# A feed-forward stage's gate and up products: product order inside a unit, and early tiles finished in turns with whole tiles

## The chip, the cores and the metric

The kernel runs on one core of a Trainium2 chip. The metric is device time in microseconds for one execution. The core has five engines, each with its own queue of instructions: TensorE (PE; its weight loads are shown as PEld), VectorE (DVE), ScalarE (ACT), GpSimd (POOL) and SyncE (SP), which issues the DMAs. They wait for each other by semaphores.

## The reference

Two layers of a decoder trunk on 512 tokens of width 1024, all in float32. Each layer has a feed-forward half-step, token mixing, a second feed-forward half-step and a gated per-layer embedding:

```python
def swiglu(x, w_in, w_out):
    gate, up = jnp.split(x @ w_in, 2, axis=-1)
    return (jax.nn.silu(gate) * up) @ w_out

for l in range(DEPTH):                                   # DEPTH = 2
    x = x + 0.5 * rms_norm(swiglu(rms_norm(x, ln_ffn1_pre[l]), w_ffn1_in[l], w_ffn1_out[l]), ln_ffn1_post[l])
    x = x + rms_norm(token_mixing(...), ln_mix_post[l])
    x = x + 0.5 * rms_norm(swiglu(rms_norm(x, ln_ffn2_pre[l]), w_ffn2_in[l], w_ffn2_out[l]), ln_ffn2_post[l])
    gate = jax.nn.sigmoid(rms_norm(x, ln_ple_pre[l]) @ w_ple_gate[l])
    x = x + rms_norm(gate * (p[l] @ w_ple_proj[l]), ln_ple_post[l])
```

The hidden width is 2816, so `x @ w_in` is 512 x 1024 times 1024 x 5632. The change lies in this product and in the SwiGLU behind it, four times in a run.

## The kernel before

**The stage.** `ffn(l, w, after)` computes gate and up for 22 tiles of 128 hidden channels (m = 0 to 21), then `ffn_out` multiplies by `w_out`. For one tile, gate and up (two rows of blocks), the halves of the 1024 inputs (two columns of blocks) and the halves L and H of the 512 tokens make a 2 x 2 by 2 x 2 block product. It is done with seven block products in place of eight, numbered 1 to 7 in `right`, from sums of weight blocks and sums of token blocks. Products 1 and 2 use the gate's plain weights, 4 uses a part of the up weights, 7 and 5 use the two halves of a first weight sum (`sx`, split into the tile w75), 6 and 3 those of a second sum (`sy`, split into w63) that is built from the first. Products 4, 6 and 7 read the token sums `tx`.

**One product.** Each float32 operand is split in two parts of type fp32r: ScalarE copies the high part (L141), VectorE subtracts to get the low part (L142). `mm3` (L169 to L171) multiplies high by high, high by low and low by high. A product is 4 x 3 = 12 matmuls of 256 columns. Its first two matmuls need the high part of the weights alone, the third needs the low part.

**Early and whole tiles.** While the normalized tokens of a stage are still being turned (`turn`, transposes named xtp), TensorE has only a part of the tokens. For the first G = 8 tiles products 1 and 2 are done in that time (`one` and `two`) from the weights w1; their sum is kept in `gates`. The seven products of these tiles are finished later by `unit(m, ...)`, which does 3 to 7 alone. I call these the early units, 0 to 7. For tiles 8 to 21 `gate` first does products 1 and 2 from a split of the gate's weights (w12) and then `unit` does the rest: whole units.

**VectorE in a unit.** L386 makes the first sum; L388 and L389 make the second; L142 makes the low parts of w75, w63, the weights of product 4 (w4) and, in a whole unit, w12. L397 adds product 6, L400 adds products 7 and 5, L403 (whole units) adds product 2, L405 adds product 3, L406 and L409 finish up, L413 multiplies by the Silu of the gate that ScalarE made (L407).

**Loads and buffers.** The raw weights (wr) come by DMA from SP's queue into slots of the pool `q`; the first three tiles' are loaded ahead. Split weights have six buffers, the sums two, PSUM banks are taken in a fixed cycle (`mmoa` for p12 and p4, `brrr` for p63 and p75).

**Who sets the order.** The source's order is a start only. The kernel is built with `schedule_with_timeline_sim=True`: a scheduler lays out the instructions of each engine from its own estimate of their times. So the rows of a unit are mixed with those of its neighbours, and a change in one place can move rows elsewhere. What each engine runs is then fixed.

Of the kernel before, what the change touches and what calls it, by code (L numbers as in the profile page):

```python
# [20 lines left out]
NM = DFF // 128  # L21
EPS = 1e-6
SLOT = 2048
NQ, NH, NW = 6, 6, 3
G, GF = 8, 3
BANKS = {"m": 2, "r": 3}
MAINL, AUXL = "mmoa", "brrr"

# [44 lines left out]
class Trunk:  # L73
# [57 lines left out]
    def bank(self, tag, name):  # L131
        return self.ps.tile([128, 512], F32, tag=tag, name=name, bufs=BANKS.get(tag, 1))

# [67 lines left out]
    def prenorm(self, t, gain, ffn=False):  # L201
        nc = self.nc
        v_, a_, g_ = nc.vector, nc.scalar, nc.gpsimd
        hs = [slice(0, 512), slice(512, 1024)]
        ss = [self.ssq(self.x[:, t, h], "ss_pre", dve=self.first and i == 1) for i, h in enumerate(hs)]
        r = self.rms(ss)
        xn = self.tmp.tile([128, D], F32, tag="xn", name="xn", bufs=1)
        for h in hs:
            v_.scalar_tensor_tensor(xn[:, h], self.x[:, t, h], r, gain[:, h], ALU.mult, ALU.mult)
        return lambda: self.turn(t, xn, ffn)  # L210

    def turn(self, t, xn, ffn):
        nc = self.nc
        v_, a_, g_ = nc.vector, nc.scalar, nc.gpsimd
# [119 lines left out]
    def ffn(self, l, w, after):  # L334


        nc, tc = self.nc, self.tc
        v_, a_, g_ = nc.vector, nc.scalar, nc.gpsimd
        post = self.gain(f"ln_ffn{w}_post", l)
        xs = (self.xh, self.xl)  # L340
        L, H = slice(0, 256), slice(256, 512)
        plain = lambda ks, ts: [q[:, ks, ts] for q in xs]
        tx = [[q[:, 0], q[:, 1]] for q in self.tx]
        k1, k2 = slice(0, 4), slice(4, 8)
        right = {1: plain(k1, L), 2: plain(k2, L), 3: plain(k2, H), 4: tx[2], 5: plain(k1, H), 6: tx[0], 7: tx[1]}
        hs = []

        lo, hi = slice(0, 512), slice(512, 1024)

        def product(n, q, out, first=True, last=True):  # L350
            for k in range(4):
                self.mm3(out, [a[:, k * 128:(k + 1) * 128] for a in q], [b[:, k] for b in right[n]],
                         first and k == 0, last and k == 3, not (first and last))


        places = lambda m: (L, H) if m % 2 else (H, L)
        early = {}

        def one(m):
            pa = self.mm_tile("p12")  # L360
            if m % 4 == 0:
                self.ffn_a = self.slot("h", [4, 512], "gates")
            early[m] = pa, self.ffn_a[:, m % 4]
            product(1, self.cut(self.ffn_w1[m], lo), pa[:, L], True, False)
            a_.activation(self.ffn_a[:, m % 4, places(m)[1]], pa[:, L], AF.Copy)

        def two(m):

            pa, a = early[m]
            product(2, self.cut(self.ffn_w1[m], hi), pa[:, L], False, True)  # L370
            a_.activation(a[:, places(m)[0]], pa[:, L], AF.Copy)

        def left(m):
            r = self.ffn_raw[m] if m < GF else self.ffn_load(l, w, [m])[0]
            if m < G:
                return r, *early[m]
            return r, self.mm_tile("p12"), self.tmp.tile([128, S], F32, tag="tb0", name="gate", bufs=4)

        def gate(m, pa, a, q):
            product(1, self.cut(q, lo), pa[:, L])  # L380
            product(2, self.cut(q, hi), pa[:, H])
            a_.activation(a[:, (H, L)[m % 2]], pa[:, L], AF.Copy)

        def unit(m, r, pa, a):
            sx, sy = (self.wraw.tile([128, 1024], F32, tag="raw", name="ws") for _ in range(2))
            v_.tensor_tensor(sx.rearrange("p (i c) -> p i c", i=2), r[:, :, lo],  # L386
                             r[:, 1].rearrange("p (i c) -> p i c", i=2), ALU.add)
            v_.tensor_tensor(sy[:, lo], sx[:, hi], r[:, 0, lo], ALU.add)  # L388
            v_.tensor_tensor(sy[:, hi], sy[:, lo], r[:, 0, hi], ALU.add)  # L389
            sx, sy = self.wsplit(sx, "w75"), self.wsplit(sy, "w63")  # L390
            u2 = [self.tmp.tile([128, 512], F32R, tag="sg", name="w4") for _ in range(2)]
            self.split(u2[0], u2[1], r[:, 1, hi])
            pc, pb, pd = self.aux_tile("p63"), self.aux_tile("p75"), self.mm_tile("p4")
            b = self.tmp.tile([128, S], F32, tag="tb1", name="up", bufs=2)
            P, Q = places(m)
            product(6, self.cut(sy, lo), pc[:, L])
            v_.tensor_tensor(a[:, Q], pc[:, L], a[:, Q if m < G else P], ALU.add)  # L397
            product(7, self.cut(sx, lo), pb[:, P])
            product(5, self.cut(sx, hi), pb[:, Q])
            v_.tensor_tensor(b.rearrange("p (i t) -> p i t", i=2), pb.rearrange("p (i t) -> p i t", i=2),  # L400
                             a[:, None, Q].to_broadcast([128, 2, 256]), ALU.add)
            if m >= G:
                v_.tensor_tensor(a[:, P], pa[:, H], a[:, P], ALU.add)  # L403
            product(3, self.cut(sy, hi), pc[:, H])
            v_.tensor_tensor(a[:, Q], pc[:, H], b[:, Q], ALU.add)  # L405
            v_.tensor_tensor(b[:, Q], pb[:, Q], b[:, P], ALU.add)  # L406
            a_.activation(a, a, AF.Silu)  # L407
            product(4, u2, pd[:, L])
            v_.tensor_tensor(b[:, P], b[:, P], pd[:, L], ALU.subtract)  # L409
            if m % 4 == 0:  # L410
                hs.append(self.slot("h", [8, 256], "h"))

            v_.scalar_tensor_tensor(hs[m // 4][:, m % 4 * 2:m % 4 * 2 + 2], b.rearrange("p (i t) -> p i t", i=2), -1.0,  # L413
                                    a.rearrange("p (i t) -> p i t", i=2), ALU.mult, ALU.mult)

        for m in range(G + 1):
            if m in NFL:
                self.flush(NFL[m])
            if m < G:
                one(m)  # L420
            if m:
                two(m - 1)
        self.flush()
        for m in range(NM):
            r, pa, a = left(m)
            if m >= G:
                gate(m, pa, a, self.wsplit(r[:, 0], "w12"))
            unit(m, r, pa, a)
        wo = self.ins[f"w_ffn{w}_out"]
        self.ffn_out(hs, lambda h, b: wo[l, h, b], post, 0.5, after)  # L430
# [1124 lines left out]
```

## Time and profile before

| | us |
|---|---|
| median of 3 runs (lowest to highest) | 2156.45 (2154.91 to 2157.81) |
| the profiled execution | 2158.23 |
| its span, first to last instruction | 2156.5 |
| TensorE busy | 2103.3 |
| VectorE busy | 1697.9 |
| ScalarE busy | 1015.6 |
| GpSimd busy | 219.9 |

The profile shows one execution. Times in it are microseconds from the start of the span, durations of single instructions are nanoseconds where the row says mean ns. In a row of a timeline the first number is the start, the second the duration; in brackets stands how long the engine was idle before it, and who ended that. A row of waits says which engine and line waited for which, the total, how often, and the longest. A row of a stretch gives its ends, its length, and for each engine the busy time and the number of instructions, then the clock that TensorE was granted (1.00 is full), the share of DMA time and GB/s. Names are cut to the tile's name without its number, so all seven products' PSUM tiles are "p" and all split weights "w". Matmuls overlap in the engine's pipeline: one lasts 280 ns or so, but the next starts after less than half of that.

The four feed-forward stages begin at about 15, 669, 1081 and 1735 us.

### The profile page before, as it was taken

To read this page: it belongs to the slowest core of one execution; us is meant where nothing else is said; L and a number is where in the kernel's file an instruction comes from. 1 tells how busy PE (TensorE), PEld (TensorE's weight loads), DVE (VectorE), ACT (ScalarE), POOL (GpSimd) and SP (SyncE) were. 2 spreads that over 40 slices of the span, in tenths; PEclk is the share of its full clock that TensorE was granted. 3 is DMA by queue.
4 is the path that set the end of the run, shared out by engine and by line. 5 is a ranking of instruction groups with operands and counts; after the bars stand their busy time and mean duration, and the time that the engine had idled before them with its cause. 6 is when DMAs were issued, how large, how long until landed. Compare 5 with 4: busy or idle time off the path is not lost.

```text
span 2156.5 us, 39845 instructions
## 1 busy us (share of the span) xinstructions
PE 2103.3 (98%) x16256; PEld 1953.4 (91%) x16256; DVE 1697.9 (79%) x2909; ACT 1015.6 (47%) x1685; POOL 219.9 (10%) x369
## 2 busy tenths in 40 slices
PE   7999999999999999999999999999999999999998
PEld 7999999898778999999889999998887789999996
DVE  8999977655767999977699999765557589999774
ACT  6444434446545444434564444345464464444343
POOL 1000011031211000011100000111412110000121
PEclk9999999999999999999999999999999999999999
DMA  5332124321042323225233222242220423222241
GB/s 215 120 116 99 70 87 153 116 65 55 21 155 71 137 99 118 69 79 182 92 108 125 111 79 93 86 169 94 61 64 2 157 88 138 100 97 79 82 147 66
DMA packets 72679, 219.10 MB, mean 102 GB/s; under 512 B 16304, under 2 KB 17328, under 8 KB 72496
## 3 DMA queue, kind: packets, MB, share of 16 engines
q1 hardware_dynamic: 72208, 216.03, 28.5%
q8 instruction: 128, 2.10, 0.4%
q10 hardware_dynamic: 288, 0.52, 0.1%
q14 instruction: 55, 0.45, 0.1%
HBM read 209.71 MB, written 6.82 MB: 100 GB/s over the span
## 4 chain that ended last, share of the span: by engine, by line
PE 84%; DVE 7%; ACT 4%; DMA 2%; issue 2%; POOL 1%; SPq 0%; DVEq 0%; POOLq 0%; ACTq 0%
PE y L496 21%; PE p L169 12%; PE p L171 12%; PE p L170 12%; PE pkrv L169 1%; PE pkrv L171 1%; PE pkrv L170 1%; DVE w L142 1%; PE y L171 1%; PE y L169 1%; PE y L170 1%; PE pgt L169 1%; PE pgt L171 1%; PE pgt L170 1%; PE po L1405 1%
## 5 line engine op out<-in xcount | busy, mean ns | idle before, releaser
L169 PE MATMUL p<-xh,w 128*128 128x256 f32 x1408 | 400.2, 286 | 14.1 <-DVE gates L397 5.8
L171 PE MATMUL p<-xh,w 128*128 128x256 f32 x1408 | 397.0, 284 | 3.7 <-DVE w L142 3.6
L170 PE MATMUL p<-xl,w 128*128 128x256 f32 x1408 | 398.7, 284 | 0.3 <-DVE xl L142 0.2
L169 PE MATMUL p<-tx,w 128*128 128x256 f32 x1056 | 294.2, 282 | 5.6 <-DVE ws L386 4.1
L170 PE MATMUL p<-tx,w 128*128 128x256 f32 x1056 | 292.1, 280 | 0.0
L171 PE MATMUL p<-tx,w 128*128 128x256 f32 x1056 | 289.8, 280 | 0.5 <-DVE w L142 0.5
L169 PEld LDWEIGHTS p<-xh,w 128*128 128x128 f32 x1408 | 268.8, 192 | 19.0 <-DVE gates L397 6.6
L171 PEld LDWEIGHTS p<-xh,w 128*128 128x128 f32 x1408 | 268.5, 192 | 5.1 <-DVE w L142 5.1
L170 PEld LDWEIGHTS p<-xl,w 128*128 128x128 f32 x1408 | 269.7, 192 | 1.0 <-DVE xl L142 0.9
L141 ACT ACTIVATE w<-ws 128x1024 fp32r<-128x1024 f32 x176 | 185.5, 1056 | 128.7 <-PE p L171 98.7
L142 DVE TENSOR_TENSOR w<-ws,w 128x1024 fp32r<-128x1024 f32 x176 | 214.0, 1217 | 19.4 <-ACT w L141 19.0
L169 PEld LDWEIGHTS p<-tx,w 128*128 128x128 f32 x1056 | 199.4, 189 | 8.1 <-ACT w L141 6.7
L170 PEld LDWEIGHTS p<-tx,w 128*128 128x128 f32 x1056 | 199.2, 189 | 0.0
L171 PEld LDWEIGHTS p<-tx,w 128*128 128x128 f32 x1056 | 196.3, 188 | 0.9 <-DVE w L142 0.7
L496 PE MATMUL y<-wo,hq 128*128 128x256 f32 x1536 | 193.3, 283 | 0.0
L496 PEld LDWEIGHTS y<-wo,hq 128*128 128x128 f32 x1536 | 186.4, 190 | 0.8
L141 ACT ACTIVATE w<-wr 128x512 fp32r<-128x512 f32 (+1 forms) x156 | 126.9, 816 | 108.8 <-PE p L171 61.5
L496 PE MATMUL y<-ws_r,h 128*128 128x256 f32 x672 | 158.3, 379 | 0.0
L142 DVE TENSOR_TENSOR w<-wr,w 128x512 fp32r<-128x512 f32 (+1 forms) x156 | 141.9, 915 | 9.9 <-ACT w L141 8.9
L532 POOL TENSOR_TENSOR tb<-tb,ln_ffn_post 128x512 f32<-128x512 f32 x16 | 24.4, 1558 | 1143.2 <-ACT junk L198 1143.2
L496 PEld LDWEIGHTS y<-ws_r,h 128*128 128x128 f32 x672 | 121.4, 189 | 13.8
L386 DVE TENSOR_TENSOR ws<-wr 128x1024 f32<-128x1024 f32 x88 | 107.0, 1216 | 0.1
(432 smaller groups left out, 4612.3 us busy)
## 6 DMA issues: line engine op xcount, KB each, us to landing
wr<-in_w_ffn_in SPq DMA_DIRECT2D x176, 512.0 KB, 4.1
ws_r<-in_w_ffn_out SPq DMA_DIRECT2D x56, 512.0 KB, 3.3
wo_r<-in_w_ffn_out SPq DMA_DIRECT2D x32, 512.0 KB, 3.3
w_r<-in_w_ffn_in SPq DMA_DIRECT2D x20, 512.0 KB, 3.8
pkrv_r<-in_w_rw SPq DMA_DIRECT2D x16, 512.0 KB, 3.5
wpg_r<-in_w_ple_gate SPq DMA_DIRECT2D x16, 512.0 KB, 4.0
xd<-x SPq DMA_DIRECT2D x8, 512.0 KB, 2.7
x<-xd SPq DMA_DIRECT2D x8, 512.0 KB, 3.5
```

The costliest lines, as they stand in the source:

```text
L141: self.nc.scalar.activation(hi, src, AF.Copy)
L142: (eng or self.nc.vector).tensor_tensor(lo, src, hi.bitcast(F32), ALU.subtract)
L169: mm(out, a[0], b[0], start=first, stop=False, skip_group_check=shared)
L170: mm(out, a[0], b[1], start=False, stop=False, skip_group_check=shared)
L171: mm(out, a[1], b[0], start=False, stop=last, skip_group_check=shared)
L386: v_.tensor_tensor(sx.rearrange("p (i c) -> p i c", i=2), r[:, :, lo], r[:, 1].rearrange("p (i c) -> p i c", i=2), ALU.add)
L496: nc.tensor.matmul(banks[n][:, u], x, y, start=n not in seen, stop=last and i == len(todo) - 1, skip_group_check=True)
L532: (g_ if not h or QL[0] == "1" else v_).tensor_tensor(tb, tb, gain[:, h * 512:h * 512 + 512], ALU.mult)
L1405: mm(po[0][hr[g]], kv[:, t - (t + b) % 2, 2 + g], sb, start=b == 0, stop=b == nb - 1)
```

## The change

Two things change in `ffn`. The units are taken in the order of the new table `UNITS`: the early units 3 to 7 are set between whole units, and units 16 to 21 come last as before. And within `unit` the first sum is split before the second sum is made, and products 7 and 5 are written ahead of product 6. The slots for the results (`hs`) become a dictionary, since tiles no longer come in order.

```diff
+UNITS = (0, 1, 2, 8, 9, 3, 10, 4, 11, 12, 5, 13, 6, 14, 15, 7, 16, 17, 18, 19, 20, 21)
...
-        hs = []
+        hs = {}
...
             v_.tensor_tensor(sx.rearrange("p (i c) -> p i c", i=2), r[:, :, lo],
                              r[:, 1].rearrange("p (i c) -> p i c", i=2), ALU.add)
+            w75 = self.wsplit(sx, "w75")
             v_.tensor_tensor(sy[:, lo], sx[:, hi], r[:, 0, lo], ALU.add)
             v_.tensor_tensor(sy[:, hi], sy[:, lo], r[:, 0, hi], ALU.add)
-            sx, sy = self.wsplit(sx, "w75"), self.wsplit(sy, "w63")
+            w63 = self.wsplit(sy, "w63")
...
-            product(6, self.cut(sy, lo), pc[:, L])
+            product(7, self.cut(w75, lo), pb[:, P])
+            product(5, self.cut(w75, hi), pb[:, Q])
+            product(6, self.cut(w63, lo), pc[:, L])
             v_.tensor_tensor(a[:, Q], pc[:, L], a[:, Q if m < G else P], ALU.add)
-            product(7, self.cut(sx, lo), pb[:, P])
-            product(5, self.cut(sx, hi), pb[:, Q])
...
-            product(3, self.cut(sy, hi), pc[:, H])
+            product(3, self.cut(w63, hi), pc[:, H])
...
-            if m % 4 == 0:
-                hs.append(self.slot("h", [8, 256], "h"))
+            if m // 4 not in hs:
+                hs[m // 4] = self.slot("h", [8, 256], "h")
...
-        for m in range(NM):
+        for m in UNITS:
```

The lines of the kernel shift by two or three: L142 becomes L144, L169 to L171 become L171 to L173, L386 becomes L388, L388 and L389 become L391 and L392, L397 becomes L402, L400 L403, L403 L406, L405 L408, L406 L409, L409 L412, L413 L416.

Three places show what the scheduler makes of it. The first is VectorE in the first stage, behind the first sums of units 0 to 2; wr_762 are the raw weights of the unit that comes fourth. Before, that is unit 3, an early one:

```order
L142 TENSOR_TENSOR w63_684<-ws_677,w63_684 128x1024
L386 TENSOR_TENSOR ws_765<-wr_762 128x1024
L406 TENSOR_TENSOR up_521<-p75_519,up_521 128x256
L142 TENSOR_TENSOR w4_777<-wr_762,w4_776 128x512
L405 TENSOR_TENSOR gates_259<-p63_605,up_608 128x256
L388 TENSOR_TENSOR ws_766<-ws_765,wr_762 128x512
L409 TENSOR_TENSOR up_521<-up_521,p4_520 128x256
L397 TENSOR_TENSOR gates_259<-p63_691,gates_259 128x256
L142 TENSOR_TENSOR w75_770<-ws_765,w75_770 128x1024
```

Now it is unit 8, a whole one:

```order
L388 TENSOR_TENSOR ws_795<-wr_762 128x1024
L144 TENSOR_TENSOR w63_684<-ws_677,w63_684 128x1024
L409 TENSOR_TENSOR up_521<-p75_519,up_521 128x256
L144 TENSOR_TENSOR w4_807<-wr_762,w4_806 128x512
L408 TENSOR_TENSOR gates_259<-p63_605,up_608 128x256
L391 TENSOR_TENSOR ws_796<-ws_795,wr_762 128x512
L144 TENSOR_TENSOR w12_767<-wr_762,w12_767 128x1024
L412 TENSOR_TENSOR up_521<-up_521,p4_520 128x256
```

Unit 8's first sum now stands before the split of unit 2's second sum (w63_684), and its split w12 comes in before its w75.

The second place is TensorE at the start of unit 5 in the same stage (before: p63_959 holds its products 6 and 3, p75_960 its 7 and 5; now p75_1562, with p4_1563 for its product 4). Before:

```order
L171 MATMUL p63_869<-tx_235,w63_862 128x256
L169 MATMUL p63_959<-tx_235,w63_952 128x256
L170 MATMUL p63_959<-tx_235,w63_952 128x256
L169 MATMUL p75_960<-tx_236,w75_949 128x256
L170 MATMUL p75_960<-tx_236,w75_949 128x256
L171 MATMUL p75_960<-tx_236,w75_949 128x256
```

Now:

```order
L173 MATMUL p63_1470<-tx_235,w63_1463 128x256
L171 MATMUL p4_1563<-tx_237,w4_1557 128x256
L172 MATMUL p4_1563<-tx_237,w4_1557 128x256
L171 MATMUL p75_1562<-tx_236,w75_1549 128x256
L172 MATMUL p75_1562<-tx_236,w75_1549 128x256
L173 MATMUL p75_1562<-tx_236,w75_1549 128x256
```

The two matmuls of product 6 ahead of product 7 are gone; the first of product 6 now stands behind all 24 of products 7 and 5. Units 1 and 2 keep their old beginning.

The third place is VectorE at the entry of the fourth stage, where xl and tx are parts of the tokens and w1_18520 is the early weight of tile 3, whose raw form is loaded into one of the two buffers of sums. Before:

```order
L243 TENSOR_TENSOR xr_18389<-xr_18389,tx_18649 128x512
L142 TENSOR_TENSOR w1_18520<-w1_r_18518,w1_18520 128x1024
L142 TENSOR_TENSOR xl_88<-xr_18389,xh_87 128x4x128
L142 TENSOR_TENSOR tx_18646<-tx_18649,tx_18646 128x4x128
L142 TENSOR_TENSOR w1_18525<-w1_r_18523,w1_18525 128x1024
```

Now:

```order
L245 TENSOR_TENSOR xr_18389<-xr_18389,tx_18649 128x512
L144 TENSOR_TENSOR xl_88<-xr_18389,xh_87 128x4x128
L144 TENSOR_TENSOR tx_18646<-tx_18649,tx_18646 128x4x128
L144 TENSOR_TENSOR xl_88<-xtp_18641,xh_87 128x4x128
L144 TENSOR_TENSOR tx_18647<-tx_18650,tx_18647 128x4x128
L144 TENSOR_TENSOR w1_18520<-w1_r_18518,w1_18520 128x1024
```

The split of w1_18520 moved behind four splits of tokens. With that the fourth stage has the order that the second has, before and now.

## The prediction

> **What bounds the kernel now.** I read the page first, then busy time by stretches of the feed-forward stages, then who TensorE waited for in the same stretches, then the timeline of VectorE.
>
> ```profile
> span 2156.5 us, 39845 instructions
> PE 2103.3 (98%) x16256; PEld 1953.4 (91%) x16256; DVE 1697.9 (79%) x2909; ACT 1015.6 (47%) x1685; POOL 219.9 (10%) x369
> ```
>
> Over the whole span TensorE (PE) idles only 2156.5 - 2103.3 = 53.2 us, and VectorE (DVE) seems to have a fifth of its time free. Both numbers are averages over unlike stages. I call the four feed-forward stages A (from about 15 us), B (from 669), C (from 1081) and D (from 1735). Busy time by stretches, in A: the early units 0 to 7, then whole units; then the same seven microseconds around unit 5 in A and in C; then the entry of D.
>
> ```profile
> core 0: us, PE busy (x) PEld busy (x) DVE busy (x) ACT busy (x) POOL busy (x), PEclk, DMA share, GB/s
> 53.00:116.00 63.00, 58.88 (x490) 58.00 (x489) 61.36 (x97) 28.06 (x34) 0.00 (x0) 1.00 0.32 118
> 120.00:245.00 125.00, 125.00 (x1054) 125.00 (x1053) 118.64 (x178) 59.38 (x77) 0.00 (x0) 1.00 0.25 93
> ...
> 81.00:88.00 7.00, 5.10 (x44) 4.90 (x43) 6.96 (x12) 1.55 (x2) 0.00 (x0) 1.00 0.39 150
> 1148.00:1155.00 7.00, 5.10 (x30) 4.90 (x29) 6.96 (x12) 1.38 (x2) 0.00 (x0) 0.76 0.40 150
> ...
> 1747.00:1760.00 13.00, 9.70 (x60) 8.89 (x61) 11.36 (x17) 7.59 (x16) 0.00 (x0) 0.87 0.46 157
> ```
>
> In the early units VectorE is busy 61.36 of 63 us and TensorE is short of 4.1 us: VectorE is the bound there. Over whole units TensorE has no idle time at all, and VectorE has 6.4 us in 125 to spare. What TensorE waited for in the units of A (53 to 253 us), of B (705 to 904), the row that C (1119 to 1321) has beside the same three as A, and of D (1775 to 1974), with total, times and longest:
>
> ```profile
> PE p L169 <- DVE ws L386: 1.9, 1, 1.9
> PE p L169 <- DVE gates L397: 1.4, 1, 1.4
> PE p L171 <- DVE w L142: 0.8, 1, 0.8
> ```
>
> ```profile
> PE p L169 <- DVE gates L397: 1.8, 1, 1.8
> PE p L169 <- ACT w L141: 0.5, 1, 0.5
> PE p L169 <- DVE ws L386: 0.3, 1, 0.3
> ```
>
> ```profile
> PE p L169 <- ACT w L141: 0.2, 1, 0.2
> ```
>
> ```profile
> PE p L169 <- DVE gates L397: 1.2, 1, 1.2
> PE p L171 <- DVE w L142: 0.5, 1, 0.5
> ```
>
> That is 4.1 + 2.6 + 4.3 + 1.7 = 12.7 us of idle TensorE, all at or just after the early units. This is what the change can reach by its order of units.
>
> **What one unit costs.** TensorE did 1054 matmuls in 125.00 us, 0.119 us each. An early unit has five products of 12 matmuls, 60 x 0.119 = 7.1 us; a whole unit seven products, 84 x 0.119 = 10.0 us. VectorE, from start to start in a stretch with no gap:
>
> ```profile
> 97.39 0.68 DVE L389 TENSOR_TENSOR ws<-ws,wr 128x512 f32<-128x512 f32 x1
> 97.99 0.41 DVE L397 TENSOR_TENSOR gates<-p,gates 128x256 f32<-128x256 f32 x1
> 98.32 0.40 DVE L409 TENSOR_TENSOR up<-up,p 128x256 f32<-128x256 f32 x1
> 98.65 1.21 DVE L386 TENSOR_TENSOR ws<-wr 128x1024 f32<-128x1024 f32 x1
> 99.78 0.68 DVE L400 TENSOR_TENSOR up<-p,gates 128x512 f32<-128x512 f32 x1
> ```
>
> So 512 columns cost 0.60 us, 256 cost 0.33, 1024 cost 1.13. An early unit has three operations of 1024 (L386, two splits), five of 512 (L388, L389, the split for product 4, L400, L413) and four of 256 (L397, L405, L406, L409): 3.4 + 3.0 + 1.3 = 7.7 us. A whole unit adds the split w12 and L403: 9.2 us. VectorE thus falls 0.6 us behind in each early unit and gains 0.8 in each whole one. Eight early units in a row are 4.8 us behind, and the split w12 of unit 8 (1.1) comes on top before unit 8 can start: 5.9. The idle time measured was 4.1, 2.6, 4.3 and 1.7, so the lead that VectorE brings from the entry must have been 1.8, 3.3, 1.6 and 4.2 us.
>
> **Early units spread among whole ones.** No instruction, byte or DMA is added. After units 0, 1 and 2 the debt is 1.8 us; units 8 and 9 bring it to 0.2; then each early unit adds 0.6 and each whole unit takes 0.8: 0.8, 0.0, 0.6, -0.2, -1.0, -0.4 and so on, so it never exceeds 1.8 again. The worst place is the start of unit 8, whose split w12 VectorE now does before its other work for unit 8 (the order shows it): 1.8 + 1.1 = 2.9. With the leads above that leaves waits of 1.1 us in A, 0 in B, 1.3 in C, and 0 in D. To these I add 0.5 us for each stage, 2.0 in all, for small waits in the alternating stretch, where one early and one whole unit are 17.1 us of TensorE against 16.9 of VectorE; the row it is nearest to is the 0.5 us wait of B. Its ends are 0 and, with 1.9 us a stage (the longest wait above), 7.6. Residue 4.4 us, so this part gains 12.7 - 4.4 = 8.3 us (2.7 to 10.3).
>
> **Products 7 and 5 first.** In the order of before VectorE and ScalarE already split the first sum (w75) ahead of the second; only TensorE began most units with two matmuls of product 6, which need w63. The longest wait of A is one, since ScalarE's split of the second sum was late:
>
> ```profile
> 83.96 0.39 PE L169 MATMUL p<-tx,w 128*128 128x256 f32 x1 [1.90 <-DVE ws L386]
> ```
>
> Starting with product 7 gives w63 the length of 24 matmuls, 24 x 0.119 = 2.9 us, more time. TensorE's work stays the same. L397, which needs product 6, comes 2.9 us later, and with it L400, L405 and the Silu; who waits then is VectorE, behind L402 in the new numbering. I count no gain of its own, because the debt above is a matter of VectorE's total, and no loss: its cover is that VectorE's next splits stand ahead of L402. If that cover is gone it costs TensorE up to 0.8 us a place, see the rivals.
>
> **DMA and buffers.** Each unit still loads its own two halves once. SP's queue differs in two rows only: at the entry of D a load of x comes earlier and one of w1 later, as they stand at the entry of B. A load takes 4.1 us to land:
>
> ```profile
> wr<-in_w_ffn_in SPq DMA_DIRECT2D x176, 512.0 KB, 4.1
> ```
>
> The raw weights of unit 8 can be fetched once unit 0's are used, and by the order VectorE has some 12 us of rows (at the prices above) between that and their first use; so the loads stay hidden, and would cost their 4.1 us only where VectorE ran that far ahead. The last six units are whole ones in both orders, so the output half of each stage finds VectorE as it did before.
>
> **The entry of D.** The scheduler moves D's first VectorE and TensorE rows into the order that B has; those of B and C stay. Who TensorE waited for at the entry of B (669 to 705 us) and of D (1735 to 1775), and what ScalarE (ACT) waited for there, B's row first:
>
> ```profile
> PE p L169 <- ACT gates L371: 0.5, 1, 0.5
> PE p L169 <- ACT xh L141: 0.5, 1, 0.5
> PE xtp L220 <- DVE xn L209: 0.3, 1, 0.3
> PE p L171 <- DVE w L142: 0.3, 1, 0.3
> ```
>
> ```profile
> PE p L169 <- ACT w L141: 1.5, 1, 1.5
> PE p L169 <- ACT gates L365: 1.3, 3, 0.6
> PE p L171 <- DVE w L142: 0.8, 1, 0.8
> PE p L169 <- ACT xh L141: 0.5, 1, 0.5
> ```
>
> ```profile
> ACT w L141 <- DMA w_r<-in_w_ffn_in: 1.2, 2, 0.9
> ...
> ACT w L141 <- DMA w_r<-in_w_ffn_in: 3.4, 1, 3.4
> ```
>
> D's entry loses 4.1 us where B's loses 1.6, because a buffer for w1 is freed late and ScalarE waits 3.4 us for the load. With B's order I take 2.5 us of gain (0 to 2.5).
>
> **The clock.** In the two stretches of seven microseconds above, engines are equally busy and TensorE waited equally long, but C did 30 matmuls where A did 44: the granted clock was 0.76 there, and 14 x 0.119 = 1.7 us were lost. At D's entry 0.87 over 13 us is another 1.7. Both stand at waits that go, so I take 3.4 us (0 to 3.4). [...]
>
> **Sum.** 8.3 + 2.5 + 3.4 = 14.2 us. The profiled execution took 2158.23 us (span 2156.5), 1.8 above the median of the three runs, 2156.45; taken from the median this gives 2142.3. The rest of the program keeps its order but for some rows of layer 0's token mixing, which I take at 0 (1 us either way).
>
> **Rivals.**
> 1. The clock drops are not tied to the waits: 81 to 88 us had the same wait at full clock. Then 3.4 us stay: 2145.7. [...]
> 2. D's entry keeps its waits and its drop, since its loads may land at other times than B's: 2.5 + 1.7 stay, 2146.5.
> 3. VectorE takes its rows in order. Where a row reads a product that TensorE has not finished, the splits behind it wait too, and the lead is spent. Over A's whole units this happened already:
>
> ```profile
> DVE gate L405 <- PE p L171: 2.1, 4, 0.8
> DVE gate L397 <- PE p L171: 1.4, 4, 0.5
> ```
>
> There each whole unit won back 0.8 us; early and whole in turns win back only 0.2. Five places (units 3, 4, 5, 6, 7) in four stages are 20; at 0.4 us each 8 us come back: 2150.3. Against it: in the new order the debt is below 1 us at all of them.
> 4. The same mechanism at its worst, slower: above 14.2 / 20 = 0.7 us a place the gain is gone, and above (14.2 + 4.3) / 20 = 0.93 the kernel is measurably slower. At the longest wait, 1.9 us, it is 38 - 14.2 = 23.8 us slower, 2180. It needs VectorE and TensorE to wait for each other at every place.
> 5. The change does nothing: w75 was split first before, TensorE is 98% busy, and new waits take the place of the old. 2152 to 2158.
>
> [...]
>
> **How the numbers follow.** Forecast 0.50 at 2142 (2137 to 2145); rival 1 0.12; rival 2 0.12; rival 3 0.13; rival 4 0.04; rival 5 0.09. A difference of 0.2% (4.3 us) is about what a measurement of this kernel can tell from none. Forecast and rivals 1 to 3 are faster by more: 0.87; rival 5 is same, 0.09; rival 4 slower, 0.04. The low end, 2136, is all 12.7 + 2.5 + 3.4 us gone and 2 more for restarting matmuls after fewer waits; the high end, 2151, takes in rival 3.
>
> **What would show it.** Right: VectorE's share of a stretch of A from 53 us on is even at about 0.95; the waits for ws and gates in the units, now L388 and L402, sum below 5 us in four stages, the rest standing at unit 8 in A and C; D's entry has B's rows; no clock drop in the units of C. Wrong: waits of 0.5 us or more at each early unit from 3 on (rivals 3, 4), D's entry unchanged (2), or clock drops at other places (1).

## The result and the profile after

The changed kernel takes 2142.23 us in the median of six executions (2140.27 to 2143.61), the kernel before 2156.86 (2152.43 to 2158.41) beside it: ratio 0.9935, 95% interval 0.9924 to 0.9947, that is 14.6 us or 0.65% faster. In a later comparison the same pair gave 2144.30 against 2155.78, ratio 0.9948 (0.9936 to 0.9961), 11.5 us. The forecast was 2142, range 2136 to 2151.

The page of the profiled execution (2142.74 us, span 2141.0), the two lines that were read of before:

```profile
span 2141.0 us, 39929 instructions
PE 2095.7 (98%) x16256; PEld 1948.2 (91%) x16256; DVE 1695.4 (79%) x2909; ACT 1012.4 (47%) x1685; POOL 217.7 (10%) x369
```

The work is the same: 16256 matmuls, 2909 operations of VectorE. TensorE idles 2141.0 - 2095.7 = 45.3 us where it was 53.2. The averages over the span hardly move; the stretches do (same columns as before: engines' busy time, clock, DMA):

```profile
53.00:116.00 63.00, 62.58 (x524) 62.17 (x523) 59.91 (x93) 29.54 (x38) 0.00 (x0) 1.00 0.29 107
120.00:245.00 125.00, 124.75 (x1041) 124.30 (x1040) 121.15 (x186) 56.64 (x74) 0.00 (x0) 1.00 0.30 105
81.00:88.00 7.00, 7.00 (x61) 7.00 (x60) 6.27 (x11) 3.28 (x4) 0.00 (x0) 1.00 0.12 38
1148.00:1155.00 7.00, 7.00 (x62) 7.00 (x61) 6.85 (x11) 2.68 (x5) 0.00 (x0) 1.00 0.22 85
```

In the first stretch of stage A, which was VectorE's, TensorE does 524 matmuls in 63 us in place of 490 and misses 0.4 us in place of 4.1. The stretch now holds whole units too, and VectorE's share is even: 59.91 of 63 (95%), then 121.15 of 125 (97%). The two pieces of seven microseconds, which had 44 and 30 matmuls around unit 5, have 61 and 62; they are the same times, but other units stand there now. TensorE's waits in the units of A, B, C and D, in this order:

```profile
PE p L173 <- DVE w L144: 0.3, 1, 0.3
PE p L171 <- DVE up L409: 0.3, 1, 0.3
```

```profile
PE p L171 <- ACT w L143: 1.0, 1, 1.0
PE p L171 <- DVE up L409: 0.3, 1, 0.3
```

```profile
PE p L173 <- DVE w L144: 0.6, 1, 0.6
PE p L171 <- DVE up L409: 0.2, 1, 0.2
```

```profile
PE p L171 <- ACT w L143: 1.0, 1, 1.0
PE p L171 <- DVE up L409: 0.3, 1, 0.3
```

They sum to 4.0 us (12.7 before), and the waits for ws and gates, which were the long ones, are gone. At the entry of D stand B's rows, TensorE's first, then ScalarE's wait for the load of w1, which was 3.4 us; the last row is the stretch 12 to 25 us after the stage's first product, as the 1747 to 1760 of before:

```profile
PE p L171 <- ACT xh L143: 0.5, 1, 0.5
PE p L171 <- ACT gates L373: 0.3, 1, 0.3
PE p L173 <- DVE w L144: 0.3, 1, 0.3
PE xtp L222 <- DVE xn L211: 0.3, 1, 0.3
```

```profile
ACT w L143 <- DMA w_r<-in_w_ffn_in: 1.2, 2, 1.0
```

```profile
1737.00:1750.00 13.00, 12.29 (x97) 11.77 (x97) 12.74 (x18) 9.05 (x17) 0.00 (x0) 1.00 0.36 122
```

One thing is new. The output halves, which read the second weights (ws_r) as they land, now wait for the DMA; before, the idle time on this row was 0.0. In e10, a second profile of the changed kernel, it is 1.4. The row of the profile above:

```profile
L499 PE MATMUL y<-ws_r,h 128*128 128x256 f32 x672 | 159.0, 379 | 2.9 <-DMA ws_r<-in_w_ffn_out 2.9
```

**Where the 15.5 us between the two profiled executions (2158.23 - 2142.74) came from.** I measured each stage from the start of its first product to that of its last: A 238.4 to 235.1, B 235.0 to 232.8, C 240.2 to 234.9, D 238.6 to 232.8, together 16.6 us less; all the rest 1.1 us more. The waits first: in the units 8.7 (12.7 - 4.0), at D's entry 2.7 (3.6 to 0.9, without the 0.5 for xh that stands ahead of the stage's first product), at the other entries 0.4. Then the clock: the profiled execution of before had four stretches at half clock besides one at its end, at 601, 1151, 1622 and 1755 us, each costing 1.7; that of the changed kernel had only the one at its end. That is 6.8, of which 3.4 in the stages and 3.4 in token mixing.

A wait also costs more than its idle time. The longest wait of A before, with the matmul ahead of it and the one behind it:

```profile
81.79 0.28 PE L171 MATMUL p<-tx,w 128*128 128x256 f32 x1
83.96 0.39 PE L169 MATMUL p<-tx,w 128*128 128x256 f32 x1 [1.90 <-DVE ws L386]
84.19 0.28 PE L170 MATMUL p<-tx,w 128*128 128x256 f32 x1
```

From 81.79 to 84.19 are 2.40 us for two steps of 0.119, so 2.16 were lost where the row shows 1.90. The difference, 0.26, is 0.23 to 0.27 at each of the 19 waits of 0.24 us and more in the units of these two profiles. Six waits of the stages are gone (12 to 8 in the units, 5 to 3 at D's entry), which is 1.6 us. With it the stages come out at 8.7 + 2.7 + 0.4 + 3.4 + 1.6 = 16.8 against 16.6 measured.

In the rest the output halves, from a stage's last product to the last matmul of L499, took 4.2 us longer in all four, 2.9 of it the new idle time; the two drops of token mixing that are gone give 3.4 back. The 0.3 us that are left of the 1.1 I do not assign.

### The profile page after: what moved, and what is told of

Its sections match the earlier page's. It is cut to its first block, busy times and chain, and to the rows that moved or that the text cites. A ratio compares the mean times of both kernels' runs of the same rounds, so it can differ in the third digit from the quotient of the medians.

```text
span 2141.0 us, 39929 instructions
## 1 busy us (share of the span) xinstructions
PE 2095.7 (98%) x16256; PEld 1948.2 (91%) x16256; DVE 1695.4 (79%) x2909; ACT 1012.4 (47%) x1685; POOL 217.7 (10%) x369
## 4 chain that ended last, share of the span: by engine, by line
PE 86%; DVE 5%; ACT 4%; DMA 2%; issue 2%; POOL 1%; SPq 0%; DVEq 0%; POOLq 0%; ACTq 0%
PE y L499 21%; PE p L171 13%; PE p L173 13%; PE p L172 13%; PE y L173 1%; PE pkrv L173 1%; PE pkrv L172 1%; PE pkrv L171 1%; PE y L172 1%; PE y L171 1%; PE pgt L173 1%; PE pgt L171 1%; PE pgt L172 1%; DMA ws_r<-in_w_ffn_out 1%; PE po L1408 1%
## 5 line engine op out<-in xcount | busy, mean ns | idle before, releaser
L171 PE MATMUL p<-xh,w 128*128 128x256 f32 x1408 | 397.8, 285 | 5.2 <-ACT gates L367 1.9
L173 PE MATMUL p<-xh,w 128*128 128x256 f32 x1408 | 393.6, 284 | 2.2 <-DVE w L144 2.0
L171 PE MATMUL p<-tx,w 128*128 128x256 f32 x1056 | 292.6, 281 | 3.8 <-ACT w L143 2.0
L173 PE MATMUL p<-tx,w 128*128 128x256 f32 x1056 | 287.7, 280 | 0.3 <-DVE w L144 0.3
L171 PEld LDWEIGHTS p<-xh,w 128*128 128x128 f32 x1408 | 268.2, 191 | 8.3 <-ACT gates L367 3.1
L173 PEld LDWEIGHTS p<-xh,w 128*128 128x128 f32 x1408 | 266.8, 191 | 3.7 <-DVE w L144 3.7
L144 DVE TENSOR_TENSOR w<-ws,w 128x1024 fp32r<-128x1024 f32 x176 | 215.0, 1222 | 14.5 <-ACT w L143 13.6
L171 PEld LDWEIGHTS p<-tx,w 128*128 128x128 f32 x1056 | 198.2, 188 | 5.9 <-ACT w L143 2.7
L173 PEld LDWEIGHTS p<-tx,w 128*128 128x128 f32 x1056 | 195.2, 188 | 0.5 <-DVE w L144 0.5
L499 PE MATMUL y<-wo,hq 128*128 128x256 f32 x1536 | 195.5, 284 | 0.0
L143 ACT ACTIVATE w<-wr 128x1024 fp32r<-128x1024 f32 (+1 forms) x156 | 127.0, 816 | 132.5 <-PE p L173 82.6
L499 PEld LDWEIGHTS y<-wo,hq 128*128 128x128 f32 x1536 | 187.8, 190 | 0.8
L499 PE MATMUL y<-ws_r,h 128*128 128x256 f32 x672 | 159.0, 379 | 2.9 <-DMA ws_r<-in_w_ffn_out 2.9
L144 DVE TENSOR_TENSOR w<-wr,w 128x1024 fp32r<-128x1024 f32 (+1 forms) x156 | 142.9, 920 | 13.0 <-ACT w L143 12.5
L499 PEld LDWEIGHTS y<-ws_r,h 128*128 128x128 f32 x672 | 121.1, 189 | 17.0 <-DMA ws_r<-in_w_ffn_out 3.5
L388 DVE TENSOR_TENSOR ws<-wr 128x1024 f32<-128x1024 f32 x88 | 107.4, 1221 | 0.0
```

The lines of the kernel that those rows point to most:

```text
L143: self.nc.scalar.activation(hi, src, AF.Copy)
L144: (eng or self.nc.vector).tensor_tensor(lo, src, hi.bitcast(F32), ALU.subtract)
L171: mm(out, a[0], b[0], start=first, stop=False, skip_group_check=shared)
L173: mm(out, a[1], b[0], start=False, stop=last, skip_group_check=shared)
L499: nc.tensor.matmul(banks[n][:, u], x, y, start=n not in seen, stop=last and i == len(todo) - 1, skip_group_check=True)
```

## The experiments

All times in microseconds; each ratio is to the kernel before, run beside it (2154.6 to 2155.8 in these comparisons). "Unit waits" are TensorE's idle times over 0.15 us from the first w63 matmul of unit 1 to a stage's last product, as A / B / C / D; by this measure the kernel before has 4.1 / 2.6 / 4.1 / 1.7 = 12.5, the changed one 0.6 / 1.3 / 0.9 / 1.3 = 4.1.

| kernel | median (lowest to highest) | ratio (95%) | unit waits, sum |
|---|---|---|---|
| e0 before again | 2154.51 (2151.34 to 2157.73) | 0.9995 (0.9986 to 1.0005) | 12.4 |
| e1 order alone | 2150.88 (2146.16 to 2155.13) | 0.9977 (0.9964 to 0.9989) | 3.3 / 1.9 / 2.6 / 1.9 = 9.7 |
| e2 products alone | 2149.01 (2145.99 to 2150.45) | 0.9963 (0.9950 to 0.9976) | 0.3 / 2.7 / 1.1 / 2.7 = 6.8 |
| e3 before, w4 on GpSimd | 2151.22 (2150.17 to 2152.73) | 0.9980 (0.9971 to 0.9990) | 2.4 / 2.5 / 1.8 / 2.5 = 9.2 |
| e4 change, block of five | 2143.89 (2143.53 to 2144.51) | 0.9948 (0.9933 to 0.9963) | 0.9 / 1.5 / 0.2 / 1.5 = 4.1 |
| e6 before, w63 in halves | 2155.50 (2154.26 to 2158.20) | 1.0005 (0.9995 to 1.0014) | 12.0 |
| e7 products alone, loaded | 2181.62 (2180.16 to 2184.95) | 1.0125 (1.0110 to 1.0140) | 25.0 |
| e8 change, loaded | 2155.73 (2153.28 to 2157.60) | 1.0001 (0.9991 to 1.0010) | 9.1 |
| e5 change, w4 of units 0 to 2 on GpSimd | 2140.32 (2138.58 to 2140.82) | 0.9935 (0.9921 to 0.9949) | 0.6 / 0 / 0 / 0 = 0.6 |
| e9 change, w63 in halves | 2143.48 (2141.51 to 2145.25) | 0.9949 (0.9935 to 0.9963) | 1.9 |
| e10 change again | 2144.30 (2142.38 to 2145.09) | 0.9948 (0.9936 to 0.9961) | 4.1 |
| e11 e5 again, beside e10 | 2139.04 (2138.39 to 2141.29) | 0.9926 (0.9913 to 0.9940) | 0.6 |

**e0: the kernel before once more.** It gives the scatter, and a second profile of the same program.

> The kernel before, run again beside itself, to see its clock. If the clock drops follow the waits of 1.7 us and more in stages C and D, each execution shows a mean clock near 0.996 and the profile has drops at about 1151 and 1755 us again. If the drops are not tied to them (rival 1), their number and places differ from execution to execution, some executions have a mean clock of 0.998 or more, and the time of those is 2 to 3 us shorter.

The number of drops varies from execution to execution, as rival 1 had it: six of the ten executions have a mean clock of 0.998 or more, and their median is 2.9 us below that of the other four. In the profile drops begin at 555, 1620 and 1753 us besides one at its end; that of 1753 is at D's entry again. The same 1.9 us wait stood in stage C, but with no clock drop behind it: 43 matmuls at clock 1.00 where the first profile had 30 at 0.76.

```profile
1146.50:1153.50 7.00, 5.10 (x43) 4.90 (x43) 6.96 (x12) 1.66 (x2) 0.00 (x0) 1.00 0.42 150
```

**e1: the order of units alone.**

```diff
+UNITS = (0, 1, 2, 8, 9, 3, 10, 4, 11, 12, 5, 13, 6, 14, 15, 7, 16, 17, 18, 19, 20, 21)
...
-        for m in range(NM):
+        for m in UNITS:
```

> The new order of units alone; the unit's products stand as before (6 first). VectorE's debt as the cause: the waits of TensorE in the units fall to about 4 to 5 us in four stages, D's entry takes B's order, and the time is that of the changed kernel, 2141 to 2145 us. Rival, that it is the later use of w63 (products 7 and 5 first): the waits for ws and gates stay at 8 us or more, 2147 to 2152 us.

Only 2.8 us of the unit waits went (12.5 to 9.7), and in each of the four stages one long wait stands, at the first product of unit 4. Stage A, with one row each of VectorE, ScalarE and TensorE in order of time:

```profile
104.72 0.68 DVE L391 TENSOR_TENSOR ws<-ws,wr 128x512 f32<-128x512 f32 x1
...
105.44 1.06 ACT L143 ACTIVATE w<-ws 128x1024 fp32r<-128x1024 f32 x1 [0.84 <-DVE ws L391]
...
106.55 0.53 PE L171 MATMUL p<-tx,w 128*128 128x256 f32 x1 [1.90 <-DVE ws L388]
```

The second half of unit 4's second sum (here L391) ends at 105.4, ScalarE copies it to w63 until 106.5, and TensorE, which wants w63 first, starts at 106.55. The row names L388 because that was VectorE's next operation; what TensorE waited for is the chain sum, copy, product 6. Spreading the units does not remove this chain as long as a unit begins with it. The forecast's sum by debt, which put nearly all of the gain in the order, is refuted here; the time, 2150.88, is the rival's.

**e2: products 7 and 5 first alone,** units 0 to 21 in a row.

```diff
+            w75 = self.wsplit(sx, "w75")
...
+            product(7, self.cut(w75, lo), pb[:, P])
+            product(5, self.cut(w75, hi), pb[:, Q])
+            product(6, self.cut(w63, lo), pc[:, L])
```

> Products 7 and 5 first alone; the units run 0 to 21. VectorE's debt as the cause: eight early units in a row still leave it 4.8 us behind and w12 of unit 8 comes on top, so 9 to 12 us of waits stay in the units; D's entry takes B's order (2.5 us and a clock drop): 2148 to 2152 us. Rival, that the place of w63 was the cause: the waits in the units fall below 5 us, 2142 to 2145 us.

This part alone nearly halves the unit waits (12.5 to 6.8), between what the expectation had for VectorE's debt (9 to 12) and for the place of w63 (below 5). In A one wait of 0.3 is left. The stretch from 53 to 116 us, then the waits in the units of B:

```profile
53.00:116.00 63.00, 62.48 (x521) 61.87 (x520) 62.37 (x97) 29.58 (x36) 0.00 (x0) 1.00 0.33 119
```

```profile
PE p L173 <- DVE w L144: 1.2, 1, 1.2
PE p L171 <- ACT w L143: 1.0, 1, 1.0
PE p L171 <- DVE up L409: 0.5, 1, 0.5
```

VectorE does 97 operations in these 63 us, as before, and is busy 99% of them; it did not become faster. TensorE nevertheless does 31 matmuls more (521 against 490). That is close to the 24 matmuls by which w63 is now needed later. I read it so: the reordering gives VectorE a lead of some 2.9 us once, at the beginning of the early units, and TensorE uses it up over the eight of them. In A and C that covers nearly the whole debt. In B and D the waits are as many as before (2.7 against 2.6 and 1.7), at other places. In each of the two, 1.0 is unit 2's w63 behind ScalarE's table load, which is read at e5 below; why the lead does not remove the rest I did not settle.

**e3: less work for VectorE in the kernel before:** the low part of w4 by GpSimd in units 0 to 7.

```diff
-            self.split(u2[0], u2[1], r[:, 1, hi])
+            self.split(u2[0], u2[1], r[:, 1, hi], g_ if m < G else None)
```

> The kernel before, with the low part of product 4's weights made by GpSimd instead of VectorE in the early units 0 to 7: 0.6 us less for VectorE in each, 7.1 us a unit as for TensorE. VectorE's debt as the cause: the waits in the units fall from 12.7 to 5 us or less without the new order, 2140 to 2146 us. Rival, that the waits come from ScalarE's splits or from PSUM banks: waits stay above 9 us, 2148 us or more. If GpSimd's subtraction is too slow (its 512-column product took 1.56 us), TensorE waits at product 4 of the early units for it instead.

A miss: 9.2 us of waits and 2151.22 are the rival's numbers. But it is not a test of the debt, since the edit did not relieve VectorE. The page of e3 counts 32 VectorE operations fewer than that of the kernel before (2877 against 2909), and yet more busy time: 1702.6 us against 1697.9. Each of the 32 pieces on GpSimd overlaps one VectorE operation that took 0.2 to 1.1 us longer than its like elsewhere, 20.9 us in all, where 32 x 0.60 = 19.2 had been moved away. One pair in stage A, the same line twice, the second time beside GpSimd:

```profile
71.50 0.68 DVE L388 TENSOR_TENSOR ws<-ws,wr 128x512 f32<-128x512 f32 x1
...
74.89 2.93 POOL L142 TENSOR_TENSOR w<-wr,w 128x512 fp32r<-128x512 f32 x1 [6.46 <-ACT w L141]
77.17 1.20 DVE L388 TENSOR_TENSOR ws<-ws,wr 128x512 f32<-128x512 f32 x1
```

So whether the waits go when an early unit costs VectorE 0.6 us less is shown by no run here. The waits that are left in A stand mostly behind ScalarE's copies:

```profile
PE p L169 <- ACT w L141: 1.7, 2, 1.2
PE p L169 <- DVE gates L397: 0.7, 2, 0.5
```

**e4: the change with another spread,** four whole units, then early units 3 to 7 in a row.

```diff
-UNITS = (0, 1, 2, 8, 9, 3, 10, 4, 11, 12, 5, 13, 6, 14, 15, 7, 16, 17, 18, 19, 20, 21)
+UNITS = (0, 1, 2, 8, 9, 10, 11, 3, 4, 5, 6, 7, 12, 13, 14, 15, 16, 17, 18, 19, 20, 21)
```

> The changed kernel with its early units 3 to 7 in one block behind units 8 to 11: order 0 1 2, 8 to 11, 3 to 7, 12 to 21. By VectorE's debt: 1.8 us after unit 2, -1.4 after unit 11, 1.6 after unit 7, never above what the changed kernel has, so no wait comes back and the time is that of the changed kernel, 2141 to 2145 us. Rival, that early units must alternate with whole ones: five in a row cost what eight in a row cost, 2147 to 2150 us as with products 7 and 5 first alone.

The unit waits are the same as the change's (4.1), and its executions, 2143.53 to 2144.51, lie within those of the changed kernel in e10, 2142.38 to 2145.09. Taking turns is not needed; whole units before the block do as well, which fits debt and lead.

**e6: w63 in two halves in the kernel before,** so that product 6 can start sooner.

```diff
-            sx, sy = self.wsplit(sx, "w75"), self.wsplit(sy, "w63")
+            sx, sy = self.wsplit(sx, "w75"), self.wsplit2(sy, "w63")   # split per 512 columns
```

> The kernel before, with w63 split in two halves of 512 columns, so that product 6 can start when the first half is there: some 1.7 us earlier (0.6 of the last sum, half of ScalarE's 1.06 and of VectorE's 1.13), for 0.07 us more of VectorE in each unit. If the waits are those of a product 6 asked for too early, the waits in the units fall from 12.5 to 6 to 8 us and with D's entry the time is 2145 to 2149 us. If VectorE's debt is the cause, they stay at 12 us or more and only D's entry gains: 2150 to 2153 us.

Nothing gained in the sum of the waits (1.7 / 3.9 / 2.5 / 3.9 = 12.0) or in time. In A and C they fell by about half, as they should where product 6 is asked for too early; in B and D they rose, mostly at another operation of VectorE (L404, which was L397). The four stages together took 4.0 us less, D's entry above all, and the output halves 3.5 more. In B:

```profile
PE p L176 <- DVE gates L404: 2.3, 1, 2.3
```

Bringing one result half a copy earlier thus does not replace a lead of 24 matmuls in all four stages.

**e7 and e8: a load on VectorE,** the last sum done twice in early units (the second time writes the same values; about 0.6 us each, 19 us in all), in e2 and in the changed kernel.

```diff
             v_.tensor_tensor(sy[:, hi], sy[:, lo], r[:, 0, hi], ALU.add)
+            if m < G:
+                v_.tensor_tensor(sy[:, hi], sy[:, lo], r[:, 0, hi], ALU.add)
```

> Products 7 and 5 first, units 0 to 21 in a row, and one operation of VectorE done twice in each early unit (the last sum, 512 columns, 0.60 us), so that an early unit has 8.3 us of VectorE against 7.1 of TensorE. By debt and lead: 8 x 1.2 + 1.1 = 10.7 us, less a lead of 4.7, 6.2, 4.5 and 6.2 (that of before and 2.9 for product 7 first), leaves about 21 us of waits against 7 without the load: 2160 to 2168 us. If VectorE's throughput does not bind and only the order in which TensorE asks does, the time stays within 4 us of the kernel without the load, 2147 to 2153 us.

> The same load, 0.60 us more of VectorE in each early unit, on the changed kernel. By debt and lead: 3.6 us after unit 2, never above 3.6 later, and 4.7 with w12 of unit 8, which the leads of 4.5 to 6.2 cover: the time stays 2142 to 2146 us, so spreading the early units is worth some 18 us under this load. If throughput does not bind, 2142 to 2146 us too, and the kernel with the units in a row shows the difference; if the alternating stretch has no room, 2150 us and more.

The load costs 2181.62 - 2149.01 = 32.6 us with the early units in a row and 2155.73 - 2142.23 = 13.5 us with them spread (33.2, and 12.5 to 15.6, if each time is first set against the kernel before beside it). The stretch 53 to 116 us and the main waits in A, of e7 and then of e8 (L404 is L402 of the changed kernel):

```profile
53.00:116.00 63.00, 57.97 (x454) 55.87 (x453) 61.62 (x95) 25.80 (x32) 0.00 (x0) 0.97 0.36 131
```

```profile
PE p L171 <- ACT w L143: 4.7, 8, 1.8
```

```profile
53.00:116.00 63.00, 61.91 (x516) 61.27 (x515) 61.55 (x96) 28.87 (x37) 0.00 (x0) 1.00 0.33 118
```

```profile
PE p L171 <- DVE gates L404: 0.9, 1, 0.9
```

VectorE is full in both (61.6 of 63); TensorE does 454 matmuls in one and 516 in the other. e7's row names ScalarE because ScalarE copies the sums that VectorE finishes late: in this stretch it waited 24.6 us for L394, the doubled sum. In direction this is the debt: with eight overloaded units in a row every one of them shows, spread they are mostly paid back. Both sizes came out higher than expected, and e8's 2155.73 is in the range that its text had for an alternating stretch without room. e7's unit waits rose by 18.2 us (6.8 to 25.0); they are some 34 waits more, which by an estimate at the 0.26 of the two profiles above are 8.8 beyond the idle time; and its profiled execution had four clock drops more (6.8). That makes 33.8, enough for the 32.6. In e8 a loaded early unit falls 1.2 us behind (0.6 + 0.6) and a whole one wins back 0.8, so a part of the load shows: its unit waits rose from 4.1 to 9.1.

**e5 and e9: the waits that the change leaves.** e5 gives the low part of w4 in units 0 to 2 to GpSimd; e9 splits w63 in halves in every unit.

```diff
-            self.split(u2[0], u2[1], r[:, 1, hi])
+            self.split(u2[0], u2[1], r[:, 1, hi], g_ if m < GF else None)    # e5
...
-            w63 = self.wsplit(sy, "w63")
+            w63 = self.wsplit2(sy, "w63")                                     # e9
```

> The changed kernel with the low part of product 4's weights made by GpSimd in place of VectorE for units 0, 1 and 2 of each stage, the three early units that still stand in a row. If VectorE's work in that stretch is the limit that is left, it has 3 x 0.60 = 1.8 us less to do there, the waits in the units (4.0 us over four stages in the changed kernel, of them 1.2 at unit 2's w63 in the second and in the fourth stage) fall to about 1 us, and the time is 2139 to 2141. Rival: those waits are ScalarE's splits coming late, as happened when the same was done to the kernel before; then the waits stay at 3 to 6 us and the time at 2142 to 2146.

> The changed kernel with the second sum's split (w63) made in two halves of 512 columns in every unit, the half for product 6 first. If the 1.2 us waits at unit 2's w63 (second and fourth stage) are the length of ScalarE's one copy of 1024 columns, the first half arrives about half a copy earlier and the two waits shrink by 0.5 us or more each: 2140 to 2142. If they are VectorE's and ScalarE's queue order, nothing is gained, and 88 x 0.07 = 6 us more work of VectorE, spread over units that have 0.2 to 0.8 us to spare, leaves the time at 2142 to 2144. With units 0 to 7 in a row the same edit gained nothing (2155.5 against 2154.8).

First what the wait at unit 2's w63 is. In stage B of the changed kernel, ScalarE's rows and then TensorE's:

```profile
702.91 1.06 ACT L143 ACTIVATE w<-ws 128x1024 fp32r<-128x1024 f32 x1 [3.77 <-PE p L173]
703.99 1.28 ACT L410 ACT_TABLE_LOAD   x1
705.28 0.63 ACT L410 ACTIVATE gates<-gates 128x512 f32<-128x512 f32 x1
705.82 1.04 ACT L143 ACTIVATE w<-ws 128x1024 fp32r<-128x1024 f32 x1
...
706.91 0.39 PE L171 MATMUL p<-tx,w 128*128 128x256 f32 x1 [1.02 <-ACT w L143]
```

The stage's first Silu, with the table load that comes with it (1.28 us), stands ahead of the copy to w63; together they hold it up by 1.8 us, and TensorE waits 1.0. D has the same rows. In e5 the order is another:

```profile
702.99 2.01 ACT L143 ACTIVATE w<-ws 128x1024 fp32r<-128x1024 f32 x2 [3.41 <-PE p L173]
705.02 1.28 ACT L410 ACT_TABLE_LOAD   x1
```

Both copies come first, the table load behind them hides, and no unit wait is left in B, C and D. The number expected for e5 was met, but not by less work for VectorE. As in e3 the pieces on GpSimd each overlap a VectorE operation that takes longer, 8.1 us over the twelve, and VectorE's busy time rose from 1695.4 to 1700.2 us with 12 operations fewer. The waits of B and D were ScalarE's queue order, as the rival had it, and by these rows what removed them is that the scheduler, with a row moved to GpSimd, laid ScalarE's copies ahead. What removed C's 0.9, most of it at the split w12 of unit 15, I did not read. GpSimd needs 1.52 us for a piece that takes VectorE 0.69, and no row of TensorE's waits names it:

```profile
L144 POOL TENSOR_TENSOR w<-wr,w 128x512 fp32r<-128x512 f32 x12 | 18.2, 1519 | 114.4 <-ACT w L143 114.4
```

e9 also cut the unit waits, to 1.9, but its waits for ws_r in the output halves rose to 4.1 us, and the time is the changed kernel's.

**e10 and e11: is e5 better than the change?** Both once more, in one comparison.

> The changed kernel once more, on the same chip and in the same call as the next, so that the two can be compared directly. 2140 to 2144.

> The changed kernel with the low part of product 4's weights of units 0, 1 and 2 made by GpSimd, once more beside the changed kernel itself. Its four stages were 6.2 us shorter in the profiled execution, of which 3.4 us are unit waits that went; if that gain is in every execution the median is 2 to 5 us below the changed kernel's in this call. Rival: the earlier difference of the medians, 1.9 us between two calls, was the scatter of calls, and the two are within 1 us.

All five executions of e11 (2138.39 to 2141.29) lie below all five of e10 (2142.38 to 2145.09); the medians differ by 5.3 us. So e5's version is the fastest here, 16.7 us below the kernel before in that comparison.

e10's profile also shows that the changed kernel is not free of clock drops. The first of two stretches in token mixing (the other drop begins at 599 us):

```profile
548.00:555.00 7.00, 6.04 (x51) 4.91 (x50) 5.61 (x20) 2.71 (x9) 1.03 (x3) 0.76 0.01 2
```

## Why the prediction was right, and where it was not

- **The total** (14.2 us against 14.6 measured, 11.5 in the later comparison) and the residue in the units (4.4 against 4.0) were right. The reading that carried it, that VectorE bounds the early units and whole units pay back, is supported: VectorE's share is even at 0.95, e4 reaches the same waits with another spread, and a load costs less than half as much when spread (13.5 against 32.6). No run shows it by taking work off VectorE, since e3 did not do so. That the total fits to 0.4 us is partly luck: the next point's error cancels, the 1.6 us of six waits' restarts stood in no term but the low end, and two drops in token mixing (3.4) that no term named paid for most of what the output halves lost (4.2).
- **"Products 7 and 5 first ... I count no gain of its own"** is the step that failed. Alone it takes 5.7 us off the unit waits (e2), more than the order alone, 2.8 (e1). The step had the right number in hand, 24 matmuls or 2.9 us more time for w63, and set it to nothing because "the debt above is a matter of VectorE's total". But by the same account waits are debt minus lead, and 2.9 us are a lead, in each stage. The 8.3 us booked on the order belong to both parts: 8.4 together (12.5 - 4.1).
- **The residue's places** were wrong. I had 1.6, 0.5, 1.8 and 0.5 in A to D, standing at unit 8's w12; measured were 0.6, 1.3, 0.8 and 1.3. In A and C the wait at unit 8 is gone, by this reading through the extra lead; C's longest, 0.6, stands at w12 of unit 15, in the alternating stretch. In B and D, where the forecast had leads of 3.3 and 4.2 and so no wait, 1.0 us is ScalarE's table load ahead of a copy, which a sum of VectorE's times cannot see.
- **D's entry** was right: from the stage's first product to unit 1's first, 39.1 us became 34.8 (2.7 less waiting and one drop), with B's rows. It is no merit of the idea: e1 to e8, whatever their edit, got B's order at D too, so that the kernel before is the exception.
- **The clock.** 3.4 us forecast for the stages, and 3.4 went there in this pair of profiles. Mean granted clocks of e0's ten executions are 0.9974, of eleven of the changed kernel's 0.9984; 0.001 of 2150 is about 2 us, from figures of three digits. Rival 1 was half right: the drops are not tied to one wait, since e0 has C's wait without the drop; on the other hand no profile of a kernel whose unit waits are all 1.1 us or shorter (the change, e4, e5, e9, e10, e11) has a drop in the four stages.
- **The rest of the program at 0 (1 us either way)**: 1.1 us more, with two drops fewer (3.4) inside. Without them it is 4.5, outside the forecast's 1, nearly all of it in the output halves, where 2.9 us are idle time for the DMA. The sentence that the output half finds VectorE as before was not enough: I take it that units that end sooner reach the loads of ws_r sooner, which no run here separates.
- **Rivals 3 and 4** (lead lost while taking turns) did not happen: no wait of 0.5 us or more at units 3 to 7.

## What to carry to other kernels

Where a helper engine is overloaded in some tiles and free in others, reckon TensorE's idle time as debt minus lead, which gave 4.4 us here against 4.0 measured. Spread the overloaded tiles, and begin each with the product whose operand is ready first: the second was a lead of 24 matmuls, 2.9 us, with no work added, and price both. Then look for what sums of busy time do not show: a table load ahead of a copy in the queue cost 1.0 us in each of two stages, and the version that had the copies in front was another 5.3 us faster, 3.5 of it idle time in the units. Count the waits as well as their idle time, since each cost about 0.26 us more than it shows in the profiles of the two kernels. And when work is moved to another engine, read the first engine's busy time again: with 32 operations moved to GpSimd VectorE was no less busy (1702.6 us against 1697.9).

## What the hardware showed that I had not expected

The granted clock dropped after short waits (2.3 us at the longest), but not after each of them. In e1 the same 1.9 us wait stands in all four stages; the stretches around it in A, B, C and D (C's stretch begins inside its wait, so its engines' times differ a little):

```profile
103.00:110.00 7.00, 5.11 (x31) 4.90 (x30) 6.95 (x13) 2.21 (x3) 0.00 (x0) 0.76 0.41 152
753.00:760.00 7.00, 5.11 (x44) 4.90 (x43) 6.47 (x11) 1.69 (x2) 0.00 (x0) 1.00 0.41 152
1169.00:1176.00 7.00, 5.55 (x34) 5.55 (x35) 6.07 (x10) 1.06 (x1) 0.00 (x0) 0.76 0.41 153
1817.00:1824.00 7.00, 5.11 (x44) 4.90 (x43) 6.46 (x12) 1.69 (x2) 0.00 (x0) 1.00 0.42 152
```

Twice the clock is 0.76 over 7 us, 0.24 x 7 = 1.7 us lost, and twice it is full; and the drop that stage C of the kernel before has in one execution (1151 us) is missing in another, e0, at the same 1.9 us wait. Which of the waits will be hit I could not tell beforehand, and in token mixing the clock dropped (e10, 548 us) after no wait longer than 1.0 us. What the traces do share is how little TensorE did just before. Each drop lasts 3.41 us at half clock (in the profile of before those that begin at 601, 1151, 1622 and 1755 us), and in all 20 that begin before a program's end, over the 14 profiles, TensorE was busy for 34% to 70% of the 3.41 us ahead (62%, 44%, 70% and 38% at these four): with a wait of 1.0 to 2.3 us or two of 0.6 among them. That much idle time did not always bring a drop, as stages B and D of e1 show.
